# Weight halves of a two-layer mLSTM and differential-attention trunk: stored in DRAM by each layer's first stage and loaded ready-made by the other three

## The chip, the cores and the metric

The kernel runs on one core of a Trainium2 chip as one program. The metric is the device time of one execution in microseconds (us). A core has a matmul engine (PE, with weight loads shown as PEld), a vector engine (DVE), an activation engine (ACT), a general engine (POOL) and a queue processor (SP) that issues every DMA of this kernel. Each engine works through its own list in a fixed order, and instructions of different engines wait for each other by semaphores.

## The reference

Two equal layers over a sequence of 2048 rows of 1024 float32 values, then a final RMSNorm. One input projection feeds two head groups, and one output projection takes both:

```python
def hybrid_layer(x, norm_w, w_in, ..., w_out, lambda_init):
    h = rmsnorm(x, norm_w)
    proj = jnp.einsum('bsd,de->bse', h, w_in)              # 1024 -> 4104 columns
    mq, mk, mv, mi, mf, mz, aq, ak, av, az = jnp.split(proj, idx, axis=-1)
    qk = silu(causal_conv(concat([mq, mk]), conv_w, conv_b))
    hm = mlstm_chunkwise(q, k, mv, mi + i_bias, mf + f_bias)   # 4 heads x 128
    ym = (rmsnorm(hm) + m_skip * mq_c) * silu(mz)
    ha = diff_attention(rope(aq), rope(ak), av, lam)           # 4 heads, 2 maps of 64
    ya = rmsnorm(ha) * (1 - lambda_init) * silu(az)
    return x + jnp.einsum('bse,ed->bsd', concat([ym, ya]), w_out)
```

## The kernel before

**Split products.** The projections are computed in PE's fp32r format with both operands split into a high half and a low rest (`hi = round(v)`, `lo = v - hi`). Each product takes three matmuls: activations hi and lo with weights hi, then activations hi with weights lo. The activations' halves are the tiles `hth` and `htl` (for the output projection `yhm`, `ylm`, `yha`, `yla`), the weights' halves `wh` and `wl`.

**Stages.** The sequence is cut into four tiles of 512 rows (t = 0 to 3). A stage is one layer and one t; eight stages run one after the other, layer 0's four first. In a stage four units u (one mLSTM head and one attention head each) follow each other. A unit's projections are 6 channel groups (`proj_ch`, two weight tiles each) and the values (`proj_v`, four weight tiles; for u = 0 eight of half the use, since its wider tiles are gone through for two pairs of row blocks). The output projection (`outproj`) runs twice in a stage's course, for hh = 0 and hh = 1, in four quarters dq of two weight tiles each (e // 2 = 0 and 1). Attention over all earlier rows (`sc`, `p`, `tpa`, `ath`, `atl`, `pv`) and the mLSTM (`ml`) are interleaved with the projections. Keys and values of earlier tiles come back from DRAM (`kp`, `vp`).

**Weights.** Every stage loads every weight tile anew by `load_w`: SP issues a DMA of 256 or 264 KB into `wr`, ACT rounds `wr` to `wh`, POOL subtracts to give `wl`. `wr`, `wh` and `wl` have three buffers each, so up to three raw tiles and three split ones can be ahead of PE or in its use. That is 676 tiles in all, 80 in each layer's first stage.

**Order.** The kernel gives each piece of work a due time, and the tile framework records them in that order. A scheduler then fixes each engine's list before the run, with PE's projections, attention and mLSTM each kept in their own order. So moving one instruction can move attention work on PE's list. In the output projection both tiles of a quarter stay in use until its end:

```python
return [(0.22 if lo else 0.44, task(dq, i, e, lo)) for dq in range(4) for i in range(2)
        for lo in (0, 1) for e in es]
```

Of the kernel before, what the change touches and what calls it, by code (L numbers as in the profile page):

```python
# [13 lines left out]
F32R = mybir.dt.float32r  # L14
BF16 = mybir.dt.bfloat16
AF = mybir.ActivationFunctionType
ALU = mybir.AluOpType
AX = mybir.AxisListType

P = 128  # L20
# [32 lines left out]
def trunk_kernel(ctx, tc, x, w_ch, w_v0, w_v, w_o, nw, cw, cb, gb, mnw, msk, anw, lam,  # L53
                 fnw, rope, out, n_layers=NL, n_t=NT):
    nc = tc.nc
    V, A, G, PE, SY = nc.vector, nc.scalar, nc.gpsimd, nc.tensor, nc.sync
# [3 lines left out]
    psm = ctx.enter_context(tc.tile_pool(name="psm", bufs=1, space=bass.MemoryType.PSUM))  # L60
    dr = ctx.enter_context(tc.tile_pool(name="dr", bufs=1, space=bass.MemoryType.DRAM))

    BUFS = dict(x=4, hth=8, htl=8, wr=3, wh=3, wl=3, yhm=3, ylm=3, yha=2, yla=2, kc=1, vc=2,
                kp=3, vp=3, q=2, p=15, ath=2, atl=2, ab=2, tmp=4, xr=2, bc=2, ot=1, ytm=1,
                mq=1, mk=1, gzm=1, gza=1, vaug=2, st=1, kw=1, hs=1, hsn=1, aj=1)
    PB = dict(mm=3, sc=2, tpa=1, pv=1, ml=1)
# [1 line left out]
    def st(shape, tag, dt=F32, name=None):  # L68
        return sb.tile(shape, dt, tag=tag, name=name or tag, bufs=BUFS[tag])

# [6 lines left out]
    def f32(ap):  # L77
        return ap.bitcast(F32)
# [89 lines left out]
    def dtile(name, shape):  # L168
        return dr.tile(shape, F32, tag=name, name=name, bufs=1)
# [9 lines left out]
        return x[t * T:(t + 1) * T, :] if l == 0 else xo[l - 1][t]  # L179


    def load_w(src, n):
        wr = st([P, 528], "wr")
        SY.dma_start(wr[:, :n], src)
        wh = st([P, 528], "wh", F32R)
        A.activation(wh[:, :n], wr[:, :n], AF.Copy)  # L186
        wl = st([P, 528], "wl", F32R)
        G.tensor_tensor(wl[:, :n], wr[:, :n], f32(wh[:, :n]), op=ALU.subtract)  # L188
        return wh, wl


# [93 lines left out]
    def proj_ch(l, u, g, H, post):  # L285

        c = {}

        def hi(dc):
            def f():  # L290
                half, j = divmod(dc, 4)
                if dc == 0:
                    c["ps"] = pst("mm", [P, T])
                if j == 0:
                    c["w"] = load_w(w_ch[l, u, g, half], 512)
                w = c["w"][0][:, j * P:(j + 1) * P]
                mm(c["ps"], w, H["hh"][dc], dc == 0, False)
                mm(c["ps"], w, H["hl"][dc], False, False)
            return f

        def lo(d0):
            def f():
                for dc in (d0, d0 + 1):
                    j = dc % 4
                    mm(c["ps"], c["w"][1][:, j * P:(j + 1) * P], H["hh"][dc], False, dc == 7)
                if d0 == 6:
                    post(c["ps"])
            return f

        return [(0.44, f) for half in range(2)  # L310
                for f in [hi(4 * half + j) for j in range(4)] + [lo(4 * half + j) for j in (0, 2)]]


    def proj_v(l, t, u, H, X):

        pr = par[l]
        c = {}
# [24 lines left out]
        def task(pair, qd, tb, lo):  # L342
            n = 264 if u == 0 else 256
            src = w_v0[l, qd] if u == 0 else w_v[l, u - 1, qd]

            def f():
                if not lo and tb == (2 * pair if u == 0 else 0):
                    c["w"] = load_w(src, 2 * n)
                    if qd == 0:
                        if pair == 0:  # L350
                            begin()
                        c["ps"] = [pst("mm", [P, T]) for _ in range(2)]
                w = c["w"][lo]
                o = slice(tb * P, (tb + 1) * P)
                if u == 0:
                    ps, st0 = c["ps"][tb - 2 * pair][:, :n], True
                else:

                    ps, st0 = c["ps"][tb // 2][:, (tb % 2) * n:(tb % 2) * n + n], tb % 2 == 0
                for j in range(2):  # L360
                    dc = qd * 2 + j
                    r = w[:, j * n:(j + 1) * n]
                    if lo:
                        mm(ps, H["hh"][dc][:, o], r, False, dc == 7)
                    else:
                        mm(ps, H["hh"][dc][:, o], r, dc == 0 and st0, False)
                        mm(ps, H["hl"][dc][:, o], r, False, False)
                if lo and qd == 3:
                    if u == 0:
                        evac(c["ps"][tb - 2 * pair], slice(tb, tb + 1), n)  # L370
                    elif tb % 2 == 1:
                        evac(c["ps"][tb // 2], slice(tb - 1, tb + 1), n)
                    if tb == 3:
                        end()
            return f
# [436 lines left out]
    def outproj(l, t, hh, Xs, es=(0, 1, 2, 3), R=None):  # L812

        src = xin(l, t) if hh == 0 else xp[l][t]
        dst = xp[l][t] if hh == 0 else xo[l][t]
        c = {}

        def task(dq, i, e, lo):
            def f():
# [2 lines left out]
                    if i == 0:  # L822
                        c["w"] = {}
                if i == 0 and e // 2 not in c["w"]:
                    c["w"][e // 2] = load_w(w_o[l, hh, dq, e // 2], 512)
                j = e % 2
                w = c["w"][e // 2][lo][:, j * 256:(j + 1) * 256]
                yh, yl = Xs[e // 2]["ym" if j == 0 else "ya"]
                for b in range(2):
                    tb = 2 * i + b  # L830
                    o = slice(tb * P, (tb + 1) * P)
# [141 lines left out]
    for k in range(-1, N + 1):  # L973
# [19 lines left out]
        if cur:  # L993
            l, t, u = cur
# [15 lines left out]
            if u == NH - 1 and s < last:  # L1010
                op = outproj(l, t, 0, Xs[k - 3:k - 1])
# [63 lines left out]
    l, t = divmod(last, n_t)  # L1075
    e = fin_t[N - 1] + 7.0
    op = outproj(l, t, 0, Xs[N - 4:N - 2], R=R) + outproj(l, t, 1, Xs[N - 2:N], (0, 1, 2), R)
    xc = put(op, xc, max(xc + 36.0, e))
    op = outproj(l, t, 1, Xs[N - 2:N], (3,), R)
# [89 lines left out]
```

## Time and profile before

| | |
|---|---|
| median of 3 runs | 2855.03 us (2853.68 to 2860.54) |
| the profiled execution, its own time | 2855.48 us |
| its span, from first to last instruction | 2853.7 us |
| busy in the span: PE, DVE, ACT, POOL | 2675.9, 1873.5, 1641.3, 1422.6 us |
| mean granted clock of PE | 0.98 |
| moved by DMA | 428.91 MB, mean 150 GB/s |

Shares are averages over eight stages. PE is busy nearly throughout, so time that can be lost or won shows as PE's idle time, and the row that ended each idle stretch says who was late. "SPq" in a row is SP's queue and its times are those of issuing a DMA, not of the transfer; the transfer's time is listed as the time from issue to landing.

### The profile page before, as it was taken

The page shows a single profiled execution, that of the slowest core. Times are in us where ns is not written, and L with a number is a line of the kernel's source. Part 1 is how long each engine was busy: PE and PEld are TensorE (multiplying, and loading weights), DVE is VectorE, ACT ScalarE, POOL GpSimd, SP SyncE. Part 2 cuts the span into 40 slices and gives each one's busy share as a digit, 9 for nine tenths or more (in the row PEclk, how much of TensorE's full clock was granted, in tenths as well). Part 3 has the DMA queues.
Part 4 walks back from the last instruction along what each step waited for, and adds up shares of the span by engine and source line. Part 5 has one row for each costly group of instructions (what it writes and reads, how often), then busy time and mean ns, then how long its engine had stood idle before and what let it go on. Part 6 is the DMA issues. An engine that isn't in the chain of part 4 may idle for free. (4 is left out here: it accounts for less than half of the span.)

```text
span 2853.7 us, 49241 instructions
## 1 busy us (share of the span) xinstructions
PE 2675.9 (94%) x16692; PEld 2376.0 (83%) x16692; DVE 1873.5 (66%) x4879; ACT 1641.3 (58%) x4407; POOL 1422.6 (50%) x1182
## 2 busy tenths in 40 slices
PE   7999899989999899989999999999999999998997
PEld 6898788878888888977889888888888888887877
DVE  5656565666757757676765466666577676776684
ACT  5555465655655556655655555555465555665664
POOL 5565656535554254434446656555554545445324
PEclk9999999999999999999999999999999999999998
DMA  6645655554653444433546455665447444465232
GB/s 202 173 137 159 187 156 146 152 186 137 181 142 121 152 130 131 140 93 116 163 143 182 141 171 151 198 185 148 144 144 233 139 140 146 115 200 159 82 99 87
DMA packets 248923, 428.91 MB, mean 150 GB/s; under 512 B 30304, under 2 KB 107104, under 8 KB 248672
## 3 DMA queue, kind: packets, MB, share of 16 engines
q1 hardware_dynamic: 248672, 425.77, 50.1%
q8 instruction: 132, 2.16, 0.3%
q14 instruction: 119, 0.97, 0.1%
HBM read 312.28 MB, written 63.05 MB: 132 GB/s over the span
## 5 line engine op out<-in xcount | busy, mean ns | idle before, releaser
L188 POOL TENSOR_TENSOR wl<-wr,wh 128x512 fp32r<-128x512 f32 (+1 forms) x676 | 898.9, 1335 | 1131.2 <-PE mm L106 523.3
L186 ACT ACTIVATE wh<-wr 128x512 fp32r<-128x512 f32 (+1 forms) x676 | 423.0, 628 | 411.0 <-PE mm L106 223.3
L106 PE MATMUL mm<-hth,wh 128*128 128x512 f32 x1536 | 621.7, 405 | 1.6 <-ACT vaug L337 1.4
L106 PE MATMUL mm<-htl,wh 128*128 128x512 f32 x1536 | 610.4, 397 | 0.0
L706 DVE TENSOR_SCALAR_CACHE_REDUCE p<-sc 128x512 f32<-128x512 f32 (+3 forms) x640 | 380.4, 605 | 130.3 <-PE sc L106 115.8
L669 ACT ACTIVATE p<-p,nm 128x512 f32<-128x512 f32 (+3 forms) x640 | 413.7, 649 | 80.8 <-DVE nm L665 79.7
L106 PE MATMUL mm<-hth,wl 128*128 128x512 f32 x1536 | 442.5, 401 | 0.0
L106 PEld LDWEIGHTS mm<-hth,wh 128*128 128x128 f32 x1536 | 292.1, 190 | 60.7 <-ACT vaug L337 2.3
L106 PEld LDWEIGHTS mm<-htl,wh 128*128 128x128 f32 x1536 | 291.7, 190 | 56.9
L106 PEld LDWEIGHTS mm<-hth,wl 128*128 128x128 f32 x1536 | 285.4, 190 | 60.9
L683 DVE SCALAR_TENSOR_TENSOR p<-p,s 128x512 f32<-128x512 f32 (+2 forms) x320 | 293.3, 962 | 2.3
L106 PE MATMUL mm<-wh,hth 128*128 128x256 f32 (+1 forms) x1024 | 268.0, 292 | 19.2 <-DVE gt L339 6.7
L755 ACT ACTIVATE ath<-tpa 128x512 fp32r<-128x512 f32 x288 | 170.4, 592 | 178.2 <-PE tpa L109 176.2
L106 PE MATMUL mm<-wh,htl 128*128 128x256 f32 (+1 forms) x1024 | 263.6, 288 | 0.0
L756 DVE TENSOR_TENSOR atl<-tpa,ath 128x512 fp32r<-128x512 f32 x288 | 197.0, 684 | 88.1 <-ACT ath L755 87.2
L106 PE MATMUL sc<-kp,q 128*128 128x512 f32 x768 | 245.9, 407 | 8.6 <-DVE p L706 8.4
L106 PEld LDWEIGHTS mm<-wh,hth 128*128 128x128 f32 x1024 | 198.8, 194 | 24.7 <-issue 10.7
L106 PEld LDWEIGHTS mm<-wh,htl 128*128 128x128 f32 x1024 | 198.8, 194 | 2.6
L109 PE MATMUL tpa<-ident,p 128*128 128x128 f32 x1088 | 186.6, 278 | 5.9 <-DVE tpa L748 4.5
L400 DVE SCALAR_TENSOR_TENSOR cacc<-mm,cw,cacc 128x511 f32<-128x511 f32 (+2 forms) x192 | 141.5, 737 | 72.2 <-ACT cacc L396 68.9
L106 PE MATMUL pv<-ath,vp 128*128 128x256 f32 x768 | 178.9, 287 | 1.4 <-ACT ath L755 1.4
L106 PE MATMUL mm<-wl,hth 128*128 128x256 f32 (+1 forms) x1024 | 168.6, 293 | 0.6 <-POOL wl L188 0.6
(202 smaller groups left out, 5672.6 us busy)
## 6 DMA issues: line engine op xcount, KB each, us to landing
wr<-in_w_ch_dram SPq DMA_DIRECT2D x384, 256.0 KB, 2.7
wr<-in_w_o_dram SPq DMA_DIRECT2D x132, 256.0 KB, 2.9
q<-ab SPq DMA_DIRECT2D x256, 128.0 KB, 2.4
vp<-vd SPq DMA_DIRECT2D x48, 512.0 KB, 4.5
wr<-in_w_v_dram SPq DMA_DIRECT2D x96, 256.0 KB, 3.4
kp<-kd SPq DMA_DIRECT2D x48, 512.0 KB, 3.7
wr<-in_w_v_dram SPq DMA_DIRECT2D x64, 264.0 KB, 3.1
kc<-ab SPq DMA_DIRECT2D x256, 64.0 KB, 2.0
```

Source lines behind the costliest of these rows:

```text
L106: pin(PE.matmul(o, l, r, start=start, stop=stop, skip_group_check=True))
L109: pin(PE.transpose(o, i, ident[:n, :n]))
L186: A.activation(wh[:, :n], wr[:, :n], AF.Copy)
L188: G.tensor_tensor(wl[:, :n], wr[:, :n], f32(wh[:, :n]), op=ALU.subtract)
L400: V.scalar_tensor_tensor(out=acc[:, d:], in0=ps[:, 0:T - d], scalar=w(j), in1=acc[:, d:], op0=ALU.mult, op1=ALU.add)
L669: A.activation(pp[:, :w], pp[:, :w], AF.Exp, bias=nm[:, m:m + 1], accum_out=zc[:, m, kt:kt + 1])
L683: V.scalar_tensor_tensor(out=pc[0][kt][:, :w], in0=pc[1][kt][:, :w], scalar=s_[:, 0:1], in1=pc[0][kt][:, :w], op0=ALU.mult, op1=ALU.add)
L706: V.tensor_scalar(out=pp[:, :w], in0=ps[:, :w], scalar1=0.125, scalar2=None, op0=ALU.mult, op1=ALU.max, accum_out=c["mx"][:, m, kt:kt + 1])
L755: A.activation(ah, p2, AF.Copy)
L756: V.tensor_tensor(al, p2, f32(ah), op=ALU.subtract)
```

## The change

`load_w` takes a key that names the weight tile. The first call with a key does what it did before, writes both halves side by side into one tile `w` of 1056 columns, and has SP store `w` to a DRAM tile. Every later call with that key has SP load both halves from there in one DMA, with neither ACT nor POOL. `w` has three buffers, which take the room of the three `wh` and three `wl`. `wr` stays with three buffers, and only first calls use it.

```diff
-    BUFS = dict(x=4, hth=8, htl=8, wr=3, wh=3, wl=3, yhm=3, ylm=3, yha=2, yla=2, kc=1, vc=2,
+    BUFS = dict(x=4, hth=8, htl=8, wr=3, w=3, yhm=3, ylm=3, yha=2, yla=2, kc=1, vc=2,
...
-    def load_w(src, n):
+    w_split = {}
+
+    def load_w(src, n, key):
+
+        w = st([P, 1056], "w", F32R)
+        wh, wl = w[:, 0:n], w[:, n:2 * n]
+        if key in w_split:
+            SY.dma_start(f32(w[:, 0:2 * n]), w_split[key])
+            return wh, wl
         wr = st([P, 528], "wr")
-        SY.dma_start(wr[:, :n], src)
-        wh = st([P, 528], "wh", F32R)
-        A.activation(wh[:, :n], wr[:, :n], AF.Copy)
-        wl = st([P, 528], "wl", F32R)
-        G.tensor_tensor(wl[:, :n], wr[:, :n], f32(wh[:, :n]), op=ALU.subtract)
+        SY.dma_start(wr[:, 0:n], src)
+        A.activation(wh, wr[:, 0:n], AF.Copy)
+        G.tensor_tensor(wl, wr[:, 0:n], f32(wh), op=ALU.subtract)
+        w_split[key] = dtile("w_" + "_".join(map(str, key)), [P, 2 * n])
+        SY.dma_start(w_split[key], f32(w[:, 0:2 * n]))
         return wh, wl
...
-                    c["w"] = load_w(src, 2 * n)
+                    c["w"] = load_w(src, 2 * n, ("v", l, u, qd))
...
-                    c["w"][e // 2] = load_w(w_o[l, hh, dq, e // 2], 512)
+                    c["w"][e // 2] = load_w(w_o[l, hh, dq, e // 2], 512, ("o", l, hh, dq, e // 2))
```

Of the 676 calls 160 are now first calls (80 a layer) and 516 load ready-made halves.

The first place is PE's list in an output projection (layer 0, t = 1, hh = 1, run in the course of stage t = 2), where quarter 1 begins. Before, `wh_9070`/`wl_9072` and `wh_9105`/`wl_9107` are quarter 0's two tiles, `wh_9194` and `wh_9208` are quarter 1's. The rows begin just behind the last matmul with `wl_9072` and end with the first one with `wh_9208`:

```order
L106 MATMUL mm_9133<-wl_9107,yhm_7704 128x256 x2
L106 MATMUL mm_9133<-wl_9107,yha_8280 128x256 x2
L106 MATMUL mm_9191<-wh_9194,yhm_6751 128x256
L106 MATMUL mm_9191<-wh_9194,ylm_6753 128x256
L106 MATMUL mm_9191<-wh_9194,yhm_6751 128x256
L106 MATMUL mm_9191<-wh_9194,ylm_6753 128x256
L106 MATMUL mm_9191<-wh_9194,yha_7077 128x256
L106 MATMUL mm_9191<-wh_9194,yla_7079 128x256
L106 MATMUL pv_8946<-ath_8964,vp_8421 128x256
L106 MATMUL mm_9191<-wh_9194,yha_7077 128x256
L106 MATMUL mm_9191<-wh_9194,yla_7079 128x256
L106 MATMUL mm_9191<-wh_9208,yhm_7704 128x256
```

Now the tiles are `w_8700` and `w_8731` (quarter 0), `w_8816` and `w_8826` (quarter 1), and `w_8826` lies in the buffer of `w_8700`. These are the last rows ahead of the first matmul with `w_8826`:

```order
L106 MATMUL pv_8586<-ath_8727,vp_8099 128x256
L106 MATMUL pv_8586<-atl_8728,vp_8099 128x256
L106 MATMUL pv_8586<-ath_8727,vp_8099 128x256 x2
L106 MATMUL pv_8586<-atl_8728,vp_8099 128x256
L106 MATMUL pv_8586<-ath_8727,vp_8099 128x256
L109 MATMUL tpa_8785<-ident_66,p_8173 128x128
L109 MATMUL tpa_8785<-ident_66,p_8371 128x128
L109 MATMUL tpa_8785<-ident_66,p_8173 128x128
L109 MATMUL tpa_8785<-ident_66,p_8371 128x128
L106 MATMUL sc_8912<-kp_8545,q_8514 128x512 x2
L106 MATMUL sc_8982<-kp_8547,q_8514 128x512 x2
L106 MATMUL mm_8815<-w_8826,yhm_7448 128x256
```

Attention and mLSTM work has moved in between. From the last matmul with `w_8700` to the first with `w_8826` stand 12 matmuls of the projection and 20 others (six `pv`, four `tpa`, eight `sc`, two `ml`), where before one `pv` stood beside 12 of the projection.

The second place is SP's list in layer 0's first stage, at the values of unit 1 (`wr_911` to `wr_1042` before). Before:

```order
L184 DMA wr_864<-in_w_v_dram 128x512
L184 DMA wr_911<-in_w_v_dram 128x512
L450 DMA kd0_0_0_557<-kc_532 128x1024
L526 DMA bw0_0_716<-bw_713 16x2x128
L184 DMA wr_997<-in_w_v_dram 128x512
L140 DMA lam_969<-in_lam_dram 128x256
L184 DMA wr_1042<-in_w_v_dram 128x512
```

Now (`w_864` is the tile whose raw tile is `wr_865`, and so on by one; `w_v_0_1_0_869` is its place in DRAM):

```order
L192 DMA wr_1000<-in_w_v_dram 128x512
L196 DMA w_v_0_1_0_869<-w_864 128x1024
L192 DMA wr_1046<-in_w_v_dram 128x512
L140 DMA lam_971<-in_lam_dram 128x256
L196 DMA w_v_0_1_1_917<-w_912 128x1024
L192 DMA wr_1106<-in_w_ch_dram 128x512
L196 DMA w_v_0_1_2_1004<-w_999 128x1024
L192 DMA wr_1143<-in_w_ch_dram 128x512
```

The store of a tile stands just ahead of the raw load that is three loads later, which takes the same `wr` buffer.

## Rows read from the trace of the kernel before

**Rows 1.** The page, busy time of each engine.

```profile
PE 2675.9 (94%) x16692; PEld 2376.0 (83%) x16692; DVE 1873.5 (66%) x4879; ACT 1641.3 (58%) x4407; POOL 1422.6 (50%) x1182
```

**Rows 2.** The eight stages: window, length, PE to POOL busy, clock, DMA share, GB/s.

```profile
0.00:309.00 309.00, 274.50 (x1645) 241.77 (x1646) 180.26 (x512) 170.04 (x452) 175.68 (x176) 0.98 0.59 174
309.00:619.00 310.00, 300.65 (x1876) 266.04 (x1875) 198.59 (x534) 179.52 (x485) 163.96 (x136) 1.00 0.53 157
619.00:987.00 368.00, 347.99 (x2161) 309.89 (x2161) 250.61 (x647) 218.20 (x587) 175.84 (x144) 0.97 0.51 151
987.00:1400.00 413.00, 385.74 (x2411) 342.58 (x2411) 285.41 (x718) 242.41 (x645) 182.23 (x149) 0.98 0.44 130
1400.00:1704.00 304.00, 291.78 (x1837) 261.38 (x1838) 177.69 (x487) 166.42 (x447) 166.52 (x136) 0.98 0.52 154
1704.00:2027.00 323.00, 309.05 (x1933) 273.14 (x1933) 216.06 (x556) 181.47 (x492) 176.00 (x143) 0.99 0.56 168
2027.00:2392.00 365.00, 349.59 (x2174) 309.80 (x2172) 257.75 (x652) 216.62 (x583) 178.41 (x144) 0.98 0.54 162
2392.00:2853.00 461.00, 416.64 (x2661) 371.42 (x2661) 307.12 (x778) 266.60 (x720) 203.92 (x161) 0.97 0.42 124
```

**Rows 3.** Waits of PE: for whom, us in total, times, longest.

```profile
PE pv L106 <- DVE atl L756: 52.8, 35, 5.6
...
PE mm L106 <- DVE htl L273: 14.8, 7, 4.0
PE sc L106 <- DVE p L706: 11.7, 14, 2.5
...
PE mm L106 <- POOL wl L188: 0.6, 1, 0.6
```

**Rows 4.** The page's costliest groups: busy us, mean ns | idle before.

```profile
L188 POOL TENSOR_TENSOR wl<-wr,wh 128x512 fp32r<-128x512 f32 (+1 forms) x676 | 898.9, 1335 | 1131.2 <-PE mm L106 523.3
L186 ACT ACTIVATE wh<-wr 128x512 fp32r<-128x512 f32 (+1 forms) x676 | 423.0, 628 | 411.0 <-PE mm L106 223.3
```

**Rows 5.** Timelines of DVE, POOL, PE near 1214 us: start, us, instruction.

```profile
1214.02 6.75 DVE L683 SCALAR_TENSOR_TENSOR p<-p,s 128x512 f32<-128x512 f32 x4
...
1213.92 1.29 POOL L436 TENSOR_TENSOR t<-t,ra 128x512 f32<-128x512 f32 x1
1215.18 1.72 POOL L188 TENSOR_TENSOR wl<-wr,wh 128x512 fp32r<-128x512 f32 x1
1216.85 3.37 POOL L442 TENSOR_TENSOR ab<-t,ab 128x512 fp32r<-128x512 f32 x2
...
1221.43 0.58 PE L106 MATMUL pv<-atl,vc 128*128 128x256 f32 x1 [5.54 <-DVE atl L756]
```

**Rows 6.** Timeline of DVE near 1092 us.

```profile
1091.93 1.42 DVE L683 SCALAR_TENSOR_TENSOR p<-p,s 128x512 f32<-128x512 f32 x2
```

**Rows 7.** DMA issues: count, KB each, median us from issue to landing.

```profile
wr<-in_w_ch_dram SPq DMA_DIRECT2D x384, 256.0 KB, 2.7
...
vp<-vd SPq DMA_DIRECT2D x48, 512.0 KB, 4.5
...
kp<-kd SPq DMA_DIRECT2D x48, 512.0 KB, 3.7
...
vd<-vc SPq DMA_DIRECT2D x24, 512.0 KB, 3.0
```

**Rows 8.** Timeline of PE where output projection quarter 1 begins, t = 2.

```profile
744.43 0.39 PE L106 MATMUL mm<-wl,yhm 128*128 128x256 f32 x2
...
744.90 0.28 PE L106 MATMUL mm<-wh,yhm 128*128 128x256 f32 x1
...
745.95 0.28 PE L106 MATMUL mm<-wh,yhm 128*128 128x256 f32 x1
```

**Rows 9.** Timeline of PE, unit 0's values: low halves of two tiles.

```profile
295.27 0.65 PE L106 MATMUL mm<-wl,hth 128*128 128x264 f32 x4
...
296.72 0.65 PE L106 MATMUL mm<-wl,hth 128*128 128x264 f32 x4
```

More of the change, by code (lines that the diff above doesn't have):

```diff
@@ L294, in f @@
                 if j == 0:
-                    c["w"] = load_w(w_ch[l, u, g, half], 512)
+                    c["w"] = load_w(w_ch[l, u, g, half], 512, ("c", l, u, g, half))
                 w = c["w"][0][:, j * P:(j + 1) * P]
```

## The prediction

> **What bounds the kernel now.** The page comes first: PE is busy 2675.9 us of a span of 2853.7 [rows 1], so 178 us of idle PE, and whatever the clock costs, are all that less work on other engines can win. The stages say where. Length less PE's busy time [rows 2] gives 34.5, 9.4, 20.0, 27.3, 12.2, 14.0, 15.4 and 44.4 us; the two first stages (the 1st and the 5th row) hold 47 of it and the six later ones 130. One minus the clock, times the length, summed over the rows, is some 56 us more. The waits of PE then say for whom: DVE's split of the transposed probabilities, 52.8 us in 35 waits, the split of the activations, 14.8, and the scaling of the scores, 11.7. POOL's `wl` ended PE's waits for only 0.6 us [rows 3]. So the weights' split is not what PE waits for, though it takes 898.9 us of POOL and 423.0 of ACT, and POOL sat idle ahead of it mostly until PE gave a buffer free [rows 4]. What it costs is indirect. In the longest such wait, 5.54 us, four 128x512 updates of `p` took 6.75 us on DVE, 1.69 each, while POOL ran two-input subtractions and products without a break, one of them a `wl` [rows 5]; two of the same form took 1.42 us, 0.71 each, elsewhere [rows 6]. DVE's two-input work is slowed by POOL's, and DVE is who PE waits for.
>
> **What is removed.** 516 of 676 splits go: 516 x 0.628 = 324 us of ACT and 516 x 1.335 = 689 us of POOL [rows 4]. Neither is a bound, so this is worth only what it frees on the way to PE. The three DVE waits sum to 79 us [rows 3]. I take half as gone, 40 us: in the stretch of rows 5 the `wl` was one of the four POOL instructions, yet it is the most frequent kind over the whole run. The bounds are nothing (POOL's other work or ACT is late instead) and the whole 79 with half of the 56 us of clock, 107.
>
> **What is added: bytes.** A ready-made load moves 512 KB for 256. The program's tiles sum to 136 MB of loads removed, 271 MB added, and 84 MB of stores in the first stages: 428.9 becomes 649 MB. The price of one load is not in the trace for `w`, but 512 KB loads are there: `vp` lands in 4.5 us at the median, `kp` in 3.7, against 2.7 for a 256 KB `wr` [rows 7]. I take 4.5: `vp` meets other traffic, and there is half as much again of it now. To this comes the time from PE's last use of a buffer to SP's issue, and from landing to PE. A matmul is listed as ending 0.16 us after the next one starts (0.28 us long, 0.117 apart [rows 8]); with the two reactions I take 0.4, an estimate. So 4.9 us from PE's last matmul with one tile to its first with the tile that takes the buffer; at `kp`'s 3.7 it is 4.1.
>
> **What is added: a wait.** Here lies the main cost. Before, up to three raw tiles stood ready behind three split ones, so a freed buffer was refilled by ACT in 0.63 us. Now a freed buffer is refilled from DRAM, and SP can issue that only when PE is done with the tile three loads back. Which places have less than 4.9 us between the two?
>
> *The output projection.* Both tiles of a quarter are in use until its end, so a quarter's second tile takes the buffer of the last quarter's first. Before, PE had 1.5 us there (744.43, when `wl` of the first tile was done, to 745.95 [rows 8]). The scheduler has put attention in the gap: the rows of the first place shown make 18 matmuls of 256 columns, eight `sc` of which six are twice as long, four transposes and two `ml`; at 0.117 us for 256 columns [rows 8] that is some 4.5 us. The same count for all 39 ready-made tiles of this kind gives 1.9 to 5.5 us, 3.7 in the mean. Each lacks 4.9 - 3.7 = 1.2 us: 39 x 1.2 = **47 us**. At 4.1 it is 26 (the gaps under 4.1 alone count), and nothing if attention on other engines lags and gives the load time anyway.
>
> *The values of unit 0.* A tile is used up in 1.46 us (295.27 to 296.72 [rows 9]), so two tiles give 2.9 us, and in the two stages t = 1 nothing stands between them. Each turn of three buffers lacks 4.9 - 2.9 = 2.0 us, eight tiles are 2.7 turns: 5.3 us, twice 11. In the four stages t = 2 and 3 the gap is 4.6 in the mean, which lacks 0.3 a turn, 3 us in all. In the two first stages the second pair of row blocks reads back what the first pair stored: a store of 3.0 (as `vd` [rows 7]) and a load of 4.5 with two reactions make some 8.3 us, while PE is there after four tiles, 5.8 us: 2.5 each, 5 us. **19 us** in all, about 8 at `kp`'s price.
>
> *All other tiles.* The remaining projections leave 5.7 us and more in nine cases of ten, since two tiles of 12 matmuls of 512 columns (twice 0.117 us each) are 5.6 us even without attention between. They lose only when a load lands late, or when it stands on SP behind a DMA that waits: the second tiles stand behind loads of `xr`, which wait until a store of the output has landed. I put **10 us** here, between nothing and 30. Behind each waiting `w` on SP stand the copies of `q` and `kc` and the `kp` and `vp` loads; PE shows no wait for any of these among its largest [rows 3], so I charge nothing, and if that cover is gone their delay adds to the wait for `p` and `atl`.
>
> *The first stages.* The store of a tile stands just ahead of the raw load that takes the same `wr` buffer (the second place shown). Both wait for the same subtraction, so SP loses only the issue. But 44 MB more in a stage that moves 174 GB/s at a share of 0.59 [rows 2], 295 GB/s if it were full, are 150 us of all DMA engines, and the share comes near 1. The loads' depth of six tiles covers most: **10 us** for both stages, from nothing to 44, if the stage stretches by what is over its length (54 + 44 MB at 295 GB/s are 332 us against 309, twice 22).
>
> **The sum.** 47 + 19 + 10 + 10 = 86 us of new waits, less 40 of old ones, is +46. The profiled execution took 2855.48, 1.8 more than its span and 0.4 above the median of the runs, so 2855.5 + 46 = **2901 us**. The clock's loss I leave as it is: some stalls that lower it go, others come.
>
> The Trainium skill (DMA: Bandwidth & Descriptors, Anatomy of one DMA) gives a fit for one DMA, 2.0 us plus its bytes over 436 thousand per us; for 512 KB that is 3.2 us, an estimate. It is stated for DMAs that GpSimd issues, and no row here is that short: the loads of that size have medians of 3.7 and 4.5. By it the new waits would be about 20 us and the sum some 2835; this is a variant of the first rival and no term of mine hangs on it.
>
> **Rivals.**
> - *Loads hidden, DVE freed: faster.* A mechanism of its own: POOL's `wl` slows DVE's two-input updates (1.69 against 0.71 us), and with three quarters of it gone all 79 us of DVE's waits go. It decides where a load from freed buffer to use stays at 4.1 us or less, so that only 26 + 8 = 34 us are lost. 2855.5 + 34 - 79 = 2810. For it speaks that the waits of PE name DVE; against it that POOL keeps 735 of its 1422 us, among them the two `ab` of rows 5.
> - *They cancel.* The 34 us of quick loads against the 40: 2850. For it: each term is a small part of the 178 us.
> - *DMA becomes the bound in the first stages*, and slows the later ones, whose share goes from 0.42 to 0.56 [rows 2] to about 0.6 to 0.75: the 44 us there in place of 10, and 30 for late landings in place of 10: 2901 + 54 = 2955. For it the near-full share; against it that PE's work ahead of its loads is deepest there.
> - *The change does nothing*: not possible, since the program issues the 516 loads ready-made.
>
> **How the numbers follow.** The forecast gets 0.45, faster 0.27, cancel 0.13, DMA-bound 0.15. About 0.3% (8.6 us) is what a measurement of this kernel can tell from no change: slower 0.60, same 0.13, faster 0.27. The extremes of all bounds together are 2855.5 - 107 + 34 = 2782 and, with 65 us for the output projection at a load of 5.5 and its other bounds and no gain, 2855.5 + 65 + 30 + 30 + 44 = 3025. Eight in ten lie between 2815, which the faster rival's middle falls just below, and 2965, just above the DMA-bound one. The forecast's own range is 2870 to 2930.
>
> **What would show it.** Right: `w` loads that land in 4 to 5 us; new waits of PE "mm" for the DMA of `w`, some 60 to 90 us, nearly all at second tiles of output quarters and at unit 0's values; waits for `atl` down by about half; updates of `p` near 0.7 us for most; first stages at a DMA share of 0.9 or more with nearly the same length. Wrong: waits for `w` under 30 us, which makes it faster; or a first stage longer by over 15 us, which makes it slower than I say.

## The result and the profile after

| | before | after |
|---|---|---|
| median, same chip | 2854.53 us (4 runs) | 2944.26 us (4 runs, 2941.54 to 2948.75) |
| ratio | | 1.0316, 95% interval 1.0297 to 1.0334 |
| profiled execution, its span | 2855.48, 2853.7 us | 2946.74, 2945.0 us |
| PE busy, idle in the span | 2675.9, 177.8 us | 2717.3, 227.7 us |
| granted clock | 0.980 | 0.973 |

The change makes the kernel slower by 90 us. The forecast was 2901: the side and most of the places were right, the size was half. The page of after, engines and DMA queue, against [rows 1]:

```profile
PE 2717.3 (92%) x16692; PEld 2392.2 (81%) x16692; DVE 1707.7 (58%) x4879; ACT 1370.8 (47%) x3891; POOL 741.0 (25%) x666
...
q1 hardware_dynamic: 271712, 645.52, 67.8%
```

POOL lost 682 of the 689 us priced, ACT 270 of 324, and DVE is 166 us less busy. Still PE is idle 50 us longer, and busy 41 us longer for the same 16692 matmuls. One minus the clock, times the span, gives 57 us before and 80 after; over the stretches in which PE is busy it is 46 and 67, so 21 of the 41 are clock. Of the other 20 a good part is how matmuls are listed: the last one before a stop stands at its whole length, 0.28 us for 256 columns, where one in a row of them takes 0.117 [rows 8]. PE stops 193 times for over 0.15 us in place of 122, and 71 x 0.16 is 11 us, an estimate.

The waits of PE after (for whom, us in total, times, longest), against [rows 3]:

```profile
PE pv L106 <- DVE atl L764: 27.4, 26, 3.5
PE mm L106 <- DMA w<-w_o: 26.1, 22, 3.3
PE mm L106 <- DMA w<-w_v: 24.1, 22, 5.6
PE sc L106 <- DVE p L714: 21.7, 25, 2.4
...
PE mm L106 <- DMA w<-w_c: 11.8, 12, 2.8
...
PE sc L106 <- DMA q<-ab: 10.9, 5, 3.2
PE sc L106 <- DMA kc<-ab: 9.9, 6, 3.7
PE mm L106 <- DVE htl L281: 5.9, 4, 3.2
```

The three DVE waits of [rows 3] went from 79.3 to 27.4 + 21.7 + 5.9 = 55.0: a relief of 24 us. In their place stand 62.0 us for ready-made loads (output projection, values, channel groups) and 20.8 for the copies of `q` and `kc`, which PE did not wait for before.

Landings (count, KB, median us from issue to landing), against [rows 7]:

```profile
w<-w_c SPq DMA_DIRECT2D x288, 512.0 KB, 4.1
w<-w_o SPq DMA_DIRECT2D x100, 512.0 KB, 4.2
...
w<-w_v SPq DMA_DIRECT2D x72, 512.0 KB, 3.5
...
w<-w_v SPq DMA_DIRECT2D x56, 528.0 KB, 5.1
wr<-in_w_ch_dram SPq DMA_DIRECT2D x96, 256.0 KB, 4.4
...
bc<-bw SPq DMA_DIRECT2D x32, 512.0 KB, 7.8
```

Most ready-made loads land in 4.1 to 4.2 us, between the two prices weighed, 3.7 and 4.5; the values of units 1 to 3 take 3.5 and the 528 KB of unit 0's 5.1. By the fit of the Trainium skill (DMA: Bandwidth & Descriptors, Anatomy of one DMA), which it states for DMAs that GpSimd issues, 512 KB would take 3.2, an estimate; none of these medians, all of loads that SP issues, is that short.

The update of `p` on DVE, 962 ns in the mean before, is now 791:

```profile
L691 DVE SCALAR_TENSOR_TENSOR p<-p,s 128x512 f32<-128x512 f32 (+2 forms) x320 | 237.6, 791 | 2.3
```

Where the time lies, by stage. A length runs from the first matmul with unit 0's values to that of the next stage, the last one to the last busy instruction; all are read from the traces, and each kernel's row is its difference to before (the kernels in the lower rows are the experiments'):

| us | L0 t=0 | t=1 | t=2 | t=3 | L1 t=0 | t=1 | t=2 | t=3 |
|---|---|---|---|---|---|---|---|---|
| before, length | 269.4 | 325.4 | 367.6 | 405.7 | 311.6 | 323.3 | 364.3 | 455.3 |
| after | +17.2 | +16.2 | +13.3 | -0.2 | +8.0 | +15.6 | +3.7 | +17.7 |
| one tile | +5.1 | +1.1 | -5.2 | +13.3 | +2.0 | +4.5 | -4.1 | +10.3 |
| one tile and stores | +18.7 | -0.4 | -6.4 | +12.7 | +10.5 | +3.2 | +1.4 | +13.0 |
| halves | +18.7 | +17.0 | +2.0 | -3.6 | +14.6 | +5.4 | +2.9 | +1.7 |
| shared slots | +100.2 | +0.7 | -9.8 | -5.0 | +88.3 | +1.2 | -9.2 | -3.9 |
| spread | +9.1 | +10.4 | -10.3 | -7.8 | +13.3 | +15.3 | -14.5 | -1.5 |

The first stage of before and of after, by windows (length, PE to POOL busy, clock, DMA share, GB/s), before first:

```profile
25.00:294.00 269.00, 257.09 (x1551) 227.18 (x1552) 160.97 (x458) 147.78 (x393) 155.51 (x132) 0.98 0.57 168
```

```profile
25.00:311.00 286.00, 267.19 (x1558) 232.93 (x1556) 153.68 (x459) 146.50 (x398) 150.68 (x127) 0.95 0.86 292
```

The DMA share goes to 0.86, near the full share forecast, and the clock there falls from 0.98 to 0.95.

**What a late load looks like.** The timelines of SP and then of PE in after, layer 0, t = 2 (start, us, instruction, idle before and who ended it):

```profile
823.98 0.36 SPq L858 DMA_DIRECT2D xr<-xp  x1
824.44 0.42 SPq L868 DMA_DIRECT2D xo<-xr  x1
824.95 0.97 SPq L189 DMA_DIRECT2D w<-w_c  x2
```

```profile
822.78 0.40 PE L106 MATMUL mm<-w,yha 128*128 128x256 f32 x2
...
828.18 0.66 PE L109 MATMUL tpa<-ident,p 128*128 128x128 f32 x4
831.20 0.50 PE L106 MATMUL mm<-hth,w 128*128 128x512 f32 x1 [2.35 <-DMA w<-w_c]
```

The first of the two loads is the one that PE waits for at 831.20. Its buffer was last used by the two matmuls at 822.78, listed to 823.18. SP could not issue it then: it stood for 6.1 us at the `xr` load of 823.98, until an output store had landed, and the load went out 1.8 us after its buffer was free. It also landed late, 6.2 us after its issue.

Counted for every stop of PE over 0.2 us that a landing of `w` ended, 54 stops and 61.7 us in after. In 28 of them, 23.8 us, SP sat idle right ahead of the issue, which in nearly all came with the buffer. In 26, 38.0 us, the load went out directly behind another DMA on SP, in 11 of these (16.4 us) behind an `xr` load, which itself waits for an output store to land.

Directly behind another DMA does not yet mean that the buffer had been free. Loads and matmuls follow the same order of tiles, so the last matmul in a load's buffer can be found for 52 of the stops (58.8 us). Where SP stood ready, the load went out 0.03 us after that matmul's listed end, and PE began 0.04 us after the landing. If every load had been issued that early and had taken the landing time it took, the stops would be 23 us shorter; if each had landed within 4.2 us, the median of all 516, at the issue it had, 31 us; with both, 42, and 17 would be left. These are estimates from the trace. So late issues and landings over the median hold more of the waits than the buffers by themselves.

### The profile page after: what moved, and what is told of

Same layout as the page of the kernel before. It is cut to its first block, busy times and chain, and to the rows that moved or that the text cites. A ratio compares the mean times of both kernels' runs of the same rounds, so it can differ in the third digit from the quotient of the medians.

```text
span 2945.0 us, 47912 instructions
## 1 busy us (share of the span) xinstructions
PE 2717.3 (92%) x16692; PEld 2392.2 (81%) x16692; DVE 1707.7 (58%) x4879; ACT 1370.8 (47%) x3891; POOL 741.0 (25%) x666
## 4 chain that ended last, share of the span: by engine, by line
PE 66%; DMA 16%; DVE 9%; ACT 3%; SPq 2%; issue 2%; POOL 1%; POOLq 0%; ACTq 0%; DVEq 0%
PE mm L106 47%; PE sc L106 7%; PE pv L106 5%; PE tpa L109 3%; PE ml L106 3%; DMA w<-w_o 3%; DMA w<-w_v 3%; DMA w<-w_c 2%; DMA bc<-bw 2%; DVE p L691 2%; DVE cacc L408 1%; DVE p L714 1%; DMA x<-xo 1%; SPq L453 1%; ACT p L677 1%
## 5 line engine op out<-in xcount | busy, mean ns | idle before, releaser
L106 PE MATMUL mm<-hth,w 128*128 128x512 f32 x3072 | 1025.0, 403 | 13.3 <-DMA w<-w_c 11.8
L106 PEld LDWEIGHTS mm<-hth,w 128*128 128x128 f32 x3072 | 580.2, 191 | 139.5 <-DMA w<-w_c 16.0
L106 PE MATMUL mm<-htl,w 128*128 128x512 f32 x1536 | 611.6, 398 | 0.0
L106 PE MATMUL mm<-w,hth 128*128 128x256 f32 (+1 forms) x2048 | 418.7, 293 | 30.4 <-DMA w<-w_v 24.1
L106 PEld LDWEIGHTS mm<-w,hth 128*128 128x128 f32 x2048 | 335.5, 194 | 43.4 <-DMA w<-w_v 25.9
L106 PEld LDWEIGHTS mm<-htl,w 128*128 128x128 f32 x1536 | 293.7, 191 | 54.4
L106 PE MATMUL mm<-w,yhm 128*128 128x256 f32 x1024 | 250.9, 297 | 38.8 <-DMA w<-w_o 26.1
L194 POOL TENSOR_TENSOR w<-wr,w 128x512 fp32r<-128x512 f32 (+1 forms) x160 | 209.9, 1317 | 226.0 <-ACT w L193 189.6
L106 PE MATMUL mm<-w,htl 128*128 128x256 f32 (+1 forms) x1024 | 263.3, 288 | 0.0
L106 PE MATMUL mm<-w,yha 128*128 128x256 f32 x1024 | 242.1, 289 | 1.4 <-ACT yha L634 1.4
```

Source lines behind the costliest of these rows:

```text
L106: pin(PE.matmul(o, l, r, start=start, stop=stop, skip_group_check=True))
L194: G.tensor_tensor(wl, wr[:, 0:n], f32(wh), op=ALU.subtract)
```

## The experiments

Ratios are to the kernel before, run on the same chip, with the 95% interval, and what a kernel loses is its median less that one's. Two theories were weighed first: *refill* (too few buffers, so PE waits for a DMA where a raw tile once stood ready) and *queue* (loads that wait stand on SP ahead of others, and others ahead of them). *Traffic* (the stores) and *relief* (what the freed ACT and POOL give back) had to be priced beside them. Every edit also lets the scheduler order the lists anew and no run here parts that from the edit, so small differences between two kernels can't be put down to the edit alone.

**One tile and stores.** Nothing is loaded ready-made: every call splits as before, now into the joined tile, and first calls also store:

```diff
-        if key in w_split:
-            SY.dma_start(f32(w[:, 0:2 * n]), w_split[key])
-            return wh, wl
...
         G.tensor_tensor(wl, wr[:, 0:n], f32(wh), op=ALU.subtract)
+        if key in w_split:
+            return wh, wl
```

> Undo one part: every call of load_w splits its tile on ACT and POOL as before, the first calls still store both halves, and w stays one tile of two halves in three buffers. Nothing is loaded ready-made. It does the work of the kernel before plus 160 stores of 512 KB or 528 KB in the two first stages. Refill theory (the loss of 90 us comes from w buffers that are refilled from DRAM and not by ACT out of a raw tile): near the kernel before, 2855 to 2865 us, no PE wait for the DMA of w, the first stages longer by under 10 us in sum. Traffic theory (the stores in the first stages cost what these grew by, 17 + 8 us): 2880 us, with both first stages some 12 us longer each and the others as before. Any saving of POOL or ACT work is absent here.

Measured 2901.99 us, 1.0149 (1.0110 to 1.0189), a loss of 46, above what either theory gave: half of the whole with no ready-made load at all. The stage table puts 29 us on the two first stages, and 26 on the two last ones, which store nothing. Traffic explains the one, not the other.

**One tile alone.** The last experiment without its stores: only the two halves in one tile are left of the change, and with them that this tile is claimed ahead of the raw one.

```diff
-        wh = st([P, 528], "wh", F32R)
-        wl = st([P, 528], "wl", F32R)
+        w = st([P, 1056], "w", F32R)
+        wh, wl = w[:, 0:n], w[:, n:2 * n]
```

> The kernel before with one part of the change: both halves lie in one tile w of three buffers in place of separate wh and wl. No stores, nothing loaded ready-made. The run with stores and one tile took 2902 us, 46 more than before, of which the two first stages grew by 18.7 + 10.5 us and the two last stages of the layers, which store nothing, by 12.7 + 13.0. Theory that the stores cost it all: 2855, same as before. Theory that sharing a tile (ACT can't refill the hi half until PE is done with the lo half) and a reordered list cost the rest: 2870 to 2875, with the t = 3 stages longer by some 10 us each and the first stages unchanged.

Measured 2890.16, 1.0114 (1.0082 to 1.0146): a loss of 32 us (23 to 42 by the interval) for a part that I had not priced. The first stages grow by 5 and 2, the t = 3 stages by 13 and 10. PE's waits here:

```profile
PE pv L106 <- DVE atl L759: 35.7, 29, 5.5
PE sc L106 <- DVE p L709: 32.4, 30, 4.0
...
PE pv L106 <- ACT ath L758: 14.8, 20, 1.8
PE mm L106 <- ACT w L190: 8.4, 8, 2.0
```

The wait for `p` is 32.4 against 11.7 in [rows 3]. ACT can round the next tile only when PE is done with both halves of the old one, where before the low half had a tile of its own; that this shifts ACT's and POOL's work into the attention's way is argued from these waits, not shown. The stores by themselves are then the other 13 of the 46 by the medians. By the table, whose profiled executions lie 6 us above the one median and 8 below the other, they are 26, of which 22 in the first stages; no more than this range is known.

**Halves in tiles of their own.** The change as it is, but `wh` and `wl` are separate tiles, each stored and loaded by its own DMA:

```diff
-            SY.dma_start(f32(w[:, 0:2 * n]), w_split[key])
+            for w, d in zip((wh, wl), w_split[key]):
+                SY.dma_start(f32(w), d)
```

> The changed kernel with hi and lo in tiles of their own (wh=3, wl=3, the same memory), so each half is stored and loaded by its own DMA of 256 KB and wh can be refilled while PE still uses wl. Refill theory: the hi half, which PE needs first, is issued earlier by the time of the lo matmuls (a third of a tile's use, 0.9 us for a channel tile) and lands some 1 us sooner (2.7 to 3 against 4.1), so most of the 62 us of waits for w go: 2885 to 2900. Traffic or queue theory: the same bytes and twice the issues on SP: 2944 to 2960.

Measured 2911.72, 1.0194 (1.0164 to 1.0224), a loss of 54, between what the theories gave: 36 of the 90 us are back. The waits for weights are left at 47.5:

```profile
PE mm L106 <- DMA wl<-wlo: 12.9, 13, 2.5
PE mm L106 <- DMA wh<-whv: 12.9, 13, 2.9
...
PE mm L106 <- DMA wh<-who: 7.1, 6, 1.8
PE mm L106 <- DMA wl<-wlv: 6.8, 10, 1.0
```

So the shared tile costs 32 us put into the old kernel, and 36 come back when it is taken out of the new one. The latter also brings shorter DMAs (3.0 and 3.2 us for a half of `w_c` in place of 4.1), which the run does not part from the earlier release, and whatever twice as many issues on SP cost.

**Ready-made only where there is time.** The output projection and unit 0's values are split anew each time:

```diff
+        if key[0] == "o" or key[0] == "v" and key[2] == 0:
+            return wh, wl
         w_split[key] = dtile("w_" + "_".join(map(str, key)), [P, 2 * n])
```

> Ready-made loads only where there is time to refill: the output projection (64 tiles a layer in the four stages are 32 first and 32 second tiles) and the values of unit 0 are split anew each time as before and never stored; channel groups and the values of units 1 to 3 are ready-made. Refill theory: the waits of PE for w of w_o (26.1 us) and of unit 0's part of w_v (most of 24.1) go, and with them what they cost in clock: 2944 - 48 - 10 = 2886 us. Queue theory (the loss is what stands behind waiting w loads on SP: q and kc copies, 21 us, and late issues): the 288 ready-made loads of the channel groups still block SP, so it keeps more than half of the loss: 2920 to 2935. Under both the first stages shrink a little, since 48 of 160 stores go.

Measured 2950.80, 1.0316 (1.0265 to 1.0366), above both theories: in sum nothing comes back that the interval, some 14 us to either side, could tell. The waits at the two tight places do go, and PE's stops for `w` over 0.2 us fall from 61.7 us to 33.3. But 156 more tiles than in after are split on ACT and POOL, which at the prices found below (95 to 111 us for 516) is 29 to 34 us, so this run does not say what the tight places cost. PE waits elsewhere:

```profile
PE sc L106 <- DVE p L716: 33.7, 33, 4.7
PE mm L106 <- DMA w<-w_c: 32.3, 15, 4.8
```

The waits for channel tiles, which have time, went from 11.8 to 32.3. One of the largest, on SP and then on PE:

```profile
2148.66 1.79 SPq L456 DMA_DIRECT2D kc<-ab  x3
2150.49 1.22 SPq L455 DMA_DIRECT2D q<-ab  x2
...
2158.10 0.59 SPq L456 DMA_DIRECT2D kc<-ab  x1
...
2160.51 0.43 SPq L558 DMA_DIRECT2D bc<-bw  x1
2161.04 1.87 SPq L189 DMA_DIRECT2D w<-w_c  x2
```

```profile
2149.45 1.07 PE L106 MATMUL mm<-hth,w 128*128 128x512 f32 x4
...
2171.56 0.50 PE L106 MATMUL mm<-hth,w 128*128 128x512 f32 x1 [3.97 <-DMA w<-w_c]
```

The buffer of the first of the two loads was free at 2150.52, when the last matmul of the row at 2149.45 is listed to end. From then to 2158.69 SP issued the copies of `q` and `kc`, one after the other, and after them four more DMAs, so the load went out 10.5 us late. It went out behind `bc`, a broadcast to all partitions, and took another 10.5 us to land. Counted as above, 5 such stops hold 15.3 us; of all its ready-made loads the 26 that are among the three DMAs after a `bc`, within 6 us, land in 8.0 us at the median, the others in 3.8. In all 15 stops whose load went out directly behind another DMA (32.4 of the 33.3 us) the buffer had been free for 0.9 to 11.6 us, and an issue at that moment would have left 0.9 us of them. So here the waits for `w` are the queue's.

**The copies of `q` and `kc` off SP.** Two tries, one edit each, to POOL (`G`) and to ACT (`A`, shown):

```diff
-                        SY.dma_start(f32(qc[c_][64 * d + 32 * s:64 * d + 32 * s + 32]), f32(ab[32 * c_:32 * c_ + 32]))
-                        SY.dma_start(f32(kc[64 * d + 32 * s:64 * d + 32 * s + 32, c_]),
+                        A.dma_start(f32(qc[c_][64 * d + 32 * s:64 * d + 32 * s + 32]), f32(ab[32 * c_:32 * c_ + 32]))
+                        A.dma_start(f32(kc[64 * d + 32 * s:64 * d + 32 * s + 32, c_]),
```

> The changed kernel with one edit: the sixteen-piece copies of ab into q and kc are issued by POOL, which makes the last part of ab, and no longer stand on SP behind a w load that waits for PE. Queue theory: the PE waits sc<-DMA for q and kc (10.9 + 9.9 = 20.8 us) go and SP issues w, kp and vp earlier too: 2944 - 21 to 35 = 2909 to 2923. Refill theory: only the 20.8 us can go and part of it comes back as wait for p: 2925 to 2944, with waits for w of some 60 us as before.

> The changed kernel with the copies of ab into q and kc issued by ACT and not by SP or POOL. On POOL each issue took 0.5 us of POOL and landed in 4.7 and 4.3 us in place of 2.4 and 2.0, which ruined that test. Here, if an issue costs ACT under 0.1 us: queue theory 2909 to 2923 (the 20.8 us of PE waits for q and kc go and SP is free for w, kp and vp); refill theory 2925 to 2944. If ACT in turn stands behind the wait for POOL's part of ab (1.3 us, 64 times) the softmax steps on ACT are later and PE's waits for p and atl grow: over 2944.

Measured 3048.10, 1.0672 (1.0639 to 1.0706), on POOL and 3013.87, 1.0543 (1.0509 to 1.0578), on ACT. Both are misses: the copies bring costs of their own. The rows for the `q` copies, POOL's group, ACT's, and SP's in the changed kernel (the last two give the shortest, median and longest issue in ns):

```profile
L453 POOL DMA_DIRECT2D q<-ab x256 | 126.7, 499 | 23.5 <-DMA kc<-ab 12.1 <-DMA q<-ab 9.1 <-issue 2.2
```

```profile
L453 ACTq DMA_DIRECT2D q<-ab x256: 513/601/1982, 67.1 to 2880.0; - x128
```

```profile
L453 SPq DMA_DIRECT2D q<-ab x256: 507/589/1950, 68.4 to 2809.7; - x128
```

One issue holds its engine for 0.5 to 0.6 us, and a unit has 16 close together. On the other engines the copies also landed in 4.3 to 4.9 us at the median in place of 2.0 and 2.4. And on ACT a new wait arose on SP, where the store `kd` of the finished keys stands behind copies that SP no longer issues:

```profile
SPq L458 <- DMA kc<-ab: 117.9, 41, 8.0
```

It was 6.3 us in after. PE's waits for `w` grew with it from 62.0 to 93.8 us, though no buffer and no load's size changed. Matched to their buffers as above, issues at once would spare 38 us of them, against 23 in after; the loads that PE waits for also land later (5.8 us at the median of the stops, against 4.5). That is the queue's mechanism for about half of the growth, in a run that meant to remove it; what the queue costs the changed kernel in time is not measured by these two.

**The relief.** Four runs add ACT and POOL work to the changed kernel whose result nothing uses: a copy and a subtraction after each ready-made load on its halves (the split kept), the same on constants, and each engine alone. The core of the second:

```diff
             SY.dma_start(f32(w[:, 0:2 * n]), w_split[key])
+            j = st([P, 528], "wr", name="wj")[:, 0:512].rearrange("p (a b) -> p a b", a=4)
+            idb = ident.unsqueeze(1).to_broadcast([P, 4, P])
+            A.activation(j, idb, AF.Copy)
+            G.tensor_tensor(j, j, idb, op=ALU.subtract)
```

> Add one suspected relief back: the halves are loaded ready-made as in the changed kernel, and after each such load ACT still does a copy of wh and POOL a subtraction of the size of the removed ones, into a dummy wr tile whose result nothing uses. If the relief of ACT and POOL is worth what the waits for atl, ath and htl fell or rose by (52.8 to 27.4, 6.4 to 11.9, 14.8 to 5.9: some 29 us), this is 29 us slower than the changed kernel, 2973 us, and four-row updates of p are slow again (mean near 0.96 us). If the relief is worth my 40 us: 2984. If it is worth nothing, since PE's waits only move from one cause to another: 2944 within 9. The dummy work also holds a w buffer some 2 us longer only if POOL comes after PE's last use; that would show as more PE waits for w.

> The changed kernel plus one ACT copy and one POOL subtraction of 128x512 for each ready-made load, as many as the change removed, on a constant and a dummy tile whose result nothing uses; unlike the run that kept the split, they wait for no load. If the 96 us that the kept split cost is the price of ACT and POOL time itself (relief), this takes 3030 to 3040 us again. If most of the 96 us came from ACT standing in its queue behind a copy that waits for a load to land (254 us of ACT's idle time there), this takes 2944 + 29 to 40 = 2973 to 2984. If relief is worth nothing: 2944.

> The changed kernel with one POOL subtraction of 128x512 per ready-made load whose result nothing uses, on constants; no ACT work. With both ACT and POOL work it was 114 us slower. Theory that POOL's two-input work slows DVE's updates of p (mean 971 ns against 791): most of the 114 comes back here, 3020 to 3045, with updates of p at 0.95 us or more. Theory that ACT's time is what is short: 2944 to 2970.

> The changed kernel with one ACT copy of 128x512 per ready-made load whose result nothing uses, on a constant; no POOL work. Theory that ACT's queue is what is short (324 us of copies that stand among the exponentials and ath): 2990 to 3030, with updates of p as in the changed kernel, 0.79 us. Theory that POOL against DVE is all of it: 2944 to 2960.

Measured: split kept 3040.72, 1.0650 (1.0618 to 1.0683); on constants 3058.58, 1.0707 (1.0678 to 1.0736); POOL alone 3028.22, 1.0608 (1.0588 to 1.0627); ACT alone 2993.46, 1.0476 (1.0447 to 1.0505). The first lies above all that was expected, the second above its relief theory. Less the 90 of the changed kernel itself, the added work costs 95 to 111 us there, POOL's 84 and ACT's 49 if each is added alone. These are no exact prices of the spared work. The added work stands at other places of the lists: on constants PE waits 30.0 us for `mk`, where after has 3.3 and before none. And in the run with POOL alone, where both inputs are one constant, a subtraction took 1.07 us and not the 1.335 of [rows 4], so that 537 us of POOL's work came back and not 689:

```profile
PE ml L106 <- DVE mk L397: 30.0, 7, 7.6
```

```profile
L192 POOL TENSOR_TENSOR wj<-ident 128x512 f32<-128x512 f32 x516 | 536.9, 1071 | 0.3
```

The updates of `p`, for constants, POOL alone and ACT alone (means over the same mix of four widths):

```profile
L695 DVE SCALAR_TENSOR_TENSOR p<-p,s 128x512 f32<-128x512 f32 (+2 forms) x320 | 295.3, 971 | 2.0
```

```profile
L694 DVE SCALAR_TENSOR_TENSOR p<-p,s 128x512 f32<-128x512 f32 (+2 forms) x320 | 255.6, 848 | 1.9
```

```profile
L694 DVE SCALAR_TENSOR_TENSOR p<-p,s 128x512 f32<-128x512 f32 (+2 forms) x320 | 229.5, 766 | 2.1
```

POOL's work makes them longer (791 to 848, where 950 or more was expected, and 971), ACT's does not (766). The Trainium skill (SBUF — State Buffer, SBUF: two separate sides) says that a DVE operation with two SBUF inputs and a POOL operation that reads SBUF take one port pair in turn, and that ACT has no part in it; the three rows agree with that. But ACT alone still costs 49 us, so the port is not all of the relief, as my forecast had it.

**More depth from the same memory.** Halves as above, and `wr`, `wh`, `wl` share nine slots (the edit against the run with halves):

```diff
-    BUFS = dict(x=4, hth=8, htl=8, wr=3, wh=3, wl=3, yhm=3, ylm=3, yha=2, yla=2, kc=1, vc=2,
+    BUFS = dict(x=4, hth=8, htl=8, w=9, yhm=3, ylm=3, yha=2, yla=2, kc=1, vc=2,
...
-        wh = st([P, 528], "wh", F32R)[:, 0:n]
+        wh = st([P, 528], "w", F32R, "wh")[:, 0:n]
```

> Halves in tiles of their own, and raw tiles and halves share nine slots of the same memory: a layer's first stage still has three raw and three split tiles, the later stages have four and a half ready-made tiles in place of three, since no raw tile takes a slot there. Refill theory: with a tile and a half more between PE's last use and the next, the 47 us of PE waits for w that are left with halves go nearly all; with what the saved clock gives, 2912 - 45 to 60 = 2852 to 2867, no different from the kernel before; and if the relief of ACT and POOL then shows undisturbed, some 20 us below it. Queue theory: SP still issues in order, 512 pieces of q and kc at 0.59 us each and loads that wait for a buffer stand in front of each other, so half of the 47 us stays: 2885 to 2895. Traffic theory: the bytes are the same, 2905 to 2912.

Measured 3015.25, 1.0576 (1.0549 to 1.0602), a miss in sum, and the most telling run by stage. The six later stages together are 26.0 us *shorter* than before. Their waits for weights are nearly gone; in layer 0's three, PE's largest wait of all and its largest for a weight are these:

```profile
PE pv L106 <- DVE atl L766: 12.7, 5, 3.5
...
PE mm L106 <- DMA wl<-wlc: 5.2, 2, 2.9
```

The first stages lose 100 and 88 us. There the next raw load now stands on SP right behind the store of the last tile's high half, which waits for ACT to round it, so load, rounding and store follow each other and PE waits for ACT. That the ring shared by raw tiles and halves brings this order is argued, not shown. The first stage of layer 0, SP and PE:

```profile
SPq L198 <- ACT wh L194: 91.2, 44, 5.5
```

```profile
PE mm L106 <- ACT wh L194: 45.4, 35, 5.3
```

**What the runs point to.** Halves; half of the tiles stored in a layer's first stage, the other half in its second; raw tiles keep slots of their own in these two; from the third stage on the halves go round all nine slots:

```diff
+        per = 2 if key[0] == "v" and key[2] == 0 else 1
+        first = 1 + per * (key[-1] % 2)
+        if k > 2 * per:
+            wh, wl = [w_slot(x)[:, 0:n] for x in ("wh", "wl")]
...
+        if k == first:
+            w_split[key] = [dtile("w" + x + "_".join(map(str, key)), [P, n]) for x in "hl"]
```

> What the runs point to, put together: halves in tiles of their own; half of the tiles stored in a layer's first stage and the other half in its second, by which the store traffic of one stage halves (a DMA share of some 0.7 in place of 0.88); in the third and fourth stages the ready-made halves go round the slots of wh, wl and wr in turn, four and a half tiles deep, while raw tiles keep slots of their own in the first two. By stage, against the kernel before: first stages +5 to +10 each (they were +18.7 and +14.6 with all stores), second +5 each, third -9.8 and -9.2 and fourth -5.0 and -3.9 as in the run with shared slots: in sum 2855 + 20 to 30 - 28 = 2847 to 2857, no different from the kernel before. Refill theory: no PE waits for w in the later two stages. If the relief of ACT and POOL (96 to 114 us as priced by added work) could be had in full once the loads are hidden, three quarters of it fall in these stages: some 2800. If instead half a layer's stores cost as much as all: 2875.

Measured 2867.02, 1.0053 (1.0034 to 1.0072): 15 of the 90 us are left, and it is still slower than before, by some 0.5%. The third and fourth stages win 34.1 in sum, the first and second lose 48.1. The first stage with half of the stores:

```profile
25.00:303.00 278.00, 261.36 (x1560) 227.89 (x1559) 159.07 (x459) 149.34 (x401) 152.02 (x130) 0.98 0.73 232
```

The share falls to 0.73 and the clock is back at 0.98, but splitting and storing in two stages costs nearly as much as in one (48.1 us against 55.7 in the first and second stages with halves).

## Why the prediction was right in sign and short in size

- **The gain, 40.** The DVE waits fell by 24, and POOL against DVE was real. But the relief was split over two engines, and what it is worth hangs on the rest: up to 95 to 111 us by added work while PE also waits for loads, 26 to 34 where the loads are hidden and it is counted against the kernel before. With 24 the costs of the change come to 114 us, with 95 to 111 to some 185 to 200, against the 86 of the sum; which, the runs do not tell.
- **The waits for `w`, 47 + 19 + 10.** Seen are 26.1 + 24.1 + 11.8 = 62.0 against 76. The places were right: 20 of the 22 waits for `w_o` are at second tiles and 21 of the 22 for `w_v` at unit 0. The typical landing was between my two prices. The reason was only a small part of it: gaps shorter than a load that is issued at once and lands at its median, for which I had put 47 + 19, hold 17 us. Late issues and late landings, which I had named and put at 10, hold some 42 of the 58.8 that could be matched. That 62 came near 76 is luck. The 0.4 us "from PE's last use of a buffer to SP's issue, and from landing to PE" was ample where SP stands ready (0.03 and 0.04 us beside the 0.16 of the listed end); what failed is that it supposed SP to stand ready, and each landing to take the median.
- **`q` and `kc` at nothing.** 20.8 us. I had named the cover and then trusted the absence of a wait in [rows 3], when the wait ahead of them on SP was the thing being added.
- **The first stages, 10.** They grew by 17.2 + 8.0 = 25.2, inside the bounds of 0 to 44; one tile alone makes 7.1 of it. The share rose to 0.86 and 0.83, a little under the 0.9 named as a sign. The sign of being wrong, a first stage longer by over 15 us, came with the 17.2.
- **The clock, left as it is.** Its loss rose by 22 us, 21 of them while PE is busy. Idle time alone grew by 50, close to the +46 of the sum; the 41 us of busy time are what I left out.
- **One tile, not priced.** The diff put two buffers into one and I read it as the same memory. It is 32 to 36 us, by two runs from both sides, each of them good to some 10.
- **The shortest row.** "No row here is that short", said of the fit's 3.2 us, overlooked `vd`, a store of 512 KB in 3.0 [rows 7]; no load there was.

Put in steps, the 90 us are 32 (one tile), 13 (stores, 26 by the stage table) and 44 (ready-made loads, net of their relief). The rival of a bound by DMA in the first stages gave 2955, close in time. Only 25 of the stages' 91 us lie in the first stages, but its other half, 30 us for late landings, is near the 31 found above. The rival that went faster needed hidden loads; shared slots hid them in six stages and won 26 us there, not the 79 it assumed.

What stays open: the queue's share by a run of its own, since both tries added something; why so many loads land late; what the relief is worth in the changed kernel; and how much of each difference is the scheduler's other order.

## What to carry to other kernels

Before a ready-made load replaces a local computation, look at the queue that will issue it: every DMA ahead of it that waits for something is now in its latency, and every DMA behind it in its wait. Count a merge of two tiles into one as a change of its own: the buffer then comes free with the later of the two uses, and here it cost 32 us with nothing else added. A load directly behind another DMA need not be late: look when its buffer was free. And price idle time and clock together: here 50 us of new idle time came with 41 us more of busy time for the same matmuls.

## What the runs showed of the hardware that was not expected

- Issuing is not free: a copy from or to 32 partitions held SP for 0.59 us at the median, 512 of them some 300 us, where a `w_c` load took 0.32. The Trainium skill (DMA: Bandwidth & Descriptors, Issuing engines are not separate DMA queues) calls the issue time usually small beside the DMA and the only thing that a second issuing engine saves. Here it is a quarter of the 2.4 us landing, and moving it cost the other engine about as much (0.50 us on POOL, 0.60 on ACT).
- A ready-made load among the three DMAs issued after the 512 KB broadcast `bc`, within 6 us, landed in 7.5 us at the median in after (27 loads), the others in 4.1 (489).
- The granted clock of the first stage, a mean over stretches at 2.4 and at 1.2 GHz, fell from 0.98 to 0.95 as PE's idle time there rose from 11.9 to 18.8 us (length less busy), and was 0.98 again with 16.6 in the run that spread the stores. With 21.7 us idle in the run with stores and one tile it was 0.96, so idle time alone does not set it; which waits do was not tried.
